# Attention layer: another order for the projections and the rotation of later heads, for the softmax's scaling and for the output projection

## The chip, the cores and the metric

The kernel runs on one NeuronCore of a Trainium2 chip. The metric is the device time of one execution in microseconds (us); of several runs the median is given. The engines are named PE (TensorE, matrix products, with its weight loads as PEld), DVE (VectorE), ACT (ScalarE), POOL (GpSimd) and SP (SyncE, which issues DMAs). L712 is line 712 of the kernel before.

## The reference

An encoder of two layers on a sequence of 512 tokens with 1024 features. Layer 0 mixes tokens by gated linear attention, layer 1 by grouped-query softmax attention; each is followed by a gated MLP with a width-3 convolution (2816 hidden features). The change lies in layer 1's attention alone:

```python
def attn_mixer(h, w_qkv, q_norm, k_norm, w_out, cos, sin):
    proj = h @ w_qkv                     # 8 query heads, 2 key heads, 2 value heads of 128
    q, k, v = split and reshape proj
    q = apply_rope(rmsnorm(q, q_norm), cos, sin)
    k = apply_rope(rmsnorm(k, k_norm), cos, sin)
    # per block of 128 queries and per head (4 query heads share one key head)
    s = einsum('bkgqd,bksd->bkgqs', q_blk, k) * scale
    p = softmax(s, axis=-1)
    o = einsum('bkgqs,bksd->bkgqd', p, v)
    return o @ w_out

def apply_rope(x, cos, sin):
    x1, x2 = x[..., :half], x[..., half:]
    return concatenate([x1 * cos - x2 * sin, x1 * sin + x2 * cos], axis=-1)
```

All in float32.

## The kernel before

Activations are held with features on the 128 partitions and the 512 tokens along the free axis, x as 8 such tiles. Every large product is made of three matmuls (`mm3`, L239 to L243): both factors are split into a rounded high part and the rest, and high x high, high x low and low x high are summed in PSUM.

**Weights.** `Weights` (L98 to L138) hands out halves of 128 x 1024 elements. A half needs its raw data from HBM (L113, an SP DMA of 1 MB for two halves, two buffers), then two casts on ACT (L118 for the high part, L119 for its negative) and an accumulating DMA issued by POOL (L120) that adds the raw data to the latter, which gives the low part. `half` also makes the next half of a fixed list ahead. There are three buffers for the high and three for the low parts.

**A pair of heads.** `roped` (L609 to L635) projects two heads at once into PSUM banks A and B, A holding the first halves of both heads, B the second: 2 x 8 steps of one `mm3`. Then the squares (L615, L616), their sum (L617), `scale_tok` (L594 to L607: a small matmul L598 into hs, on DVE L602, L181, a power on POOL L185, and L605 gives a scale per token and head), the four products with the norm's weight and cos or sin (L623), and per head a subtract on DVE (L630) and an add on POOL (L631), each on 64 partitions, into the rotated tile ry. `qpair` (L663) splits ry into high and low part (ACT L638, DVE L639). `kpair` (L648) does the same for the keys, with the scale multiplied in. `roped`, `kpair` and `qpair` are generators: each `yield` is a point at which the caller may go on with something else. For the keys and the query pair 0 these steps lie between each other and the value projection (L676 to L692).

**The blocks.** Query heads 0 to 7 times 4 blocks of 128 queries make 32 blocks t. In the loop at L754:

- `scores(t)`: 3 matmuls into one of two banks "s", row maximum (DVE L712), its negative scaled (L713), the exponential with its row sum (ACT L715), the reciprocal (L716) and the scaling of p by it (L717).
- a filler: 4 steps (`F_STEPS`) of the query pair that comes next, so pair 1 is prepared in blocks 0 to 7, pair 2 in 8 to 15, pair 3 in 16 to 23; what is left of a pair is done ahead of its first block (L757 to L759).
- `turn(t - 4)`: four PE transposes of p (L729) and the copy to high and low part (ACT L732, DVE L733).
- `mix(t - 6)` on every second block: p times v, 12 matmuls of 256 columns, into "po"; after a head's second, the head's output is split (oT, L638 and L639).

**The output projection** `out_steps` (L276 to L308) has a step of six matmuls (L292) per pair of output tiles and head. Of its first two groups the heads 0 to 5 come first (12 steps); the heads 6 and 7 follow, then groups 2 and 3. Before, these 12 steps are put into the loop from block 31 on, three in a block, the rest behind the loop.

The program's order is not the order on the engines: instructions are put in order per engine by a scheduler of the framework, with the program's order as the priority, and it may pull ready work ahead. Each engine then works through its list in that order and waits on semaphores.

PSUM has 8 banks: "acc" 3, "s" 2, "pt" 2, "po" 1. In SBUF "g" has 22 big buffers (128 x 1024), "t" 6 small ones (128 x 512; p and ry are there), "u" 4 (the four products of L623).

Of the kernel before, what the change touches and what calls it, by code (L numbers as in the profile page):

```python
# [1 line left out]

# [5 lines left out]
F32 = mybir.dt.float32  # L8
# [3 lines left out]
ALU = mybir.AluOpType  # L12

P = 128
S = 512
# [6 lines left out]
QH, HD = 8, 128  # L22
# [5 lines left out]

GATE_STEPS, GATE_LAG = (0, 2, 5, 7, 10, 12, 15, 17), 2

F_STEPS = 4
LAGS = (4, 6)


PC_NORM = 0
# [6 lines left out]
def hybrid_encoder_kernel(  # L42
# [21 lines left out]
    pe, act, dve, pool, sync = nc.tensor, nc.scalar, nc.vector, nc.gpsimd, nc.sync  # L64
# [8 lines left out]
    def nm(s):  # L73
        uid[0] += 1
        return f"{s}{uid[0]}"
# [9 lines left out]
    def big(dt, n):  # L85
        return pair("g", 22, dt, n)

    def tmp(tag, n, w=S):
        return sp.tile([P, w], F32, tag=tag, bufs={"u": 4, "t": 6, "sq": 3}[tag], name=nm(n))
# [63 lines left out]
    for c in range(KC):  # L153
        sync.dma_start(x[c], xT[c * P : (c + 1) * P, :])
        r = slice((c % 4) * S, (c % 4 + 1) * S)
# [120 lines left out]
    def out_steps(src, hl, nxt):  # L276


        pss, ws = {}, {}

        def part(ng, ks):
            if ng not in pss:
                pss[ng] = [bank("s" if ng % 2 else "acc", "op") for _ in range(2)]
            for k in ks:
                hf, kk = divmod(k, 4)
                if (ng, hf) not in ws:
                    ws[ng, hf] = W.half(src, ng * 2 + hf)
                wh, wl = ws[ng, hf]
                for i, (wt, mv) in enumerate(((wh, hl[k][0]), (wh, hl[k][1]), (wl, hl[k][0]))):
                    for n in range(2):  # L290
                        sl = slice((kk * 2 + n) * P, (kk * 2 + n + 1) * P)
                        mm(pss[ng][n], wt[:, sl], mv, start=k == 0 and i == 0, stop=k == KC - 1 and i == 2)  # L292
                yield

        def end(ng):
            for n in range(2):
                c = ng * 2 + n
                dve.tensor_tensor(x[c], x[c], pss[ng][n], ALU.add)
                nxt.chunk(c)

        yield from part(0, range(6))
        yield from part(1, range(6))
        for ng in range(2):
            yield from part(ng, (6, 7))
            end(ng)
        for ng in (2, 3):
            yield from part(ng, range(KC))
            end(ng)  # L308
# [278 lines left out]
    def attention(norm, nxt):  # L587
# [3 lines left out]
        cos, sin = cs[:, :S], cs[:, S:]  # L591
        r2 = cp.tile([P, NT], F32, name="r2")

        def scale_tok(sq, extra, keep):  # L594

            ps = bank("pt", "hs")
            for j in range(NT):
                mm(ps[:, 2 * j : 2 * j + 2], sq[:, j * P : (j + 1) * P], bd, start=True, stop=True)  # L598
            t = tiny(8, "hs", "tiny2")
            t3 = t.rearrange("p (j e) -> p j e", e=2)  # L600
            bc = lambda a: a.rearrange("p (j o) -> p j o", o=1).to_broadcast([P, NT, 2])
            dve.tensor_tensor(t3, ps[:, :8].rearrange("p (j e) -> p j e", e=2), bc(r2), ALU.mult)  # L602
            r = rsqrt_eps(t, 8, "hr", tag="tiny2")
            o = cp.tile([P, 8], F32, name=nm(keep))
            dve.scalar_tensor_tensor(o.rearrange("p (j e) -> p j e", e=2), r.rearrange("p (j e) -> p j e", e=2),  # L605
                                     extra, bc(norm.rtok), ALU.mult, ALU.mult)
            return o  # L607

        def roped(i, wcol, extra, keep, tag="acc"):  # L609

            pa, pb = bank(tag, "A"), bank(tag, "B")
            yield from feature_steps(*W.half(qk_order[i], 0), norm.hl, pa)
            yield from feature_steps(*W.half(qk_order[i], 1), norm.hl, pb)
            qa, qb = tmp("sq", "qa"), tmp("sq", "qb")
            act.activation(qa, pa, AF.Square)  # L615
            act.activation(qb, pb, AF.Square)  # L616
            dve.tensor_tensor(qa, qa, qb, ALU.add)  # L617
            yield
            sc = scale_tok(qa, extra, keep)
            wa, wb = prm[:, wcol : wcol + 1], prm[:, wcol + 1 : wcol + 2]  # L620
            t = [tmp("u", "rt") for _ in range(4)]
            for dst, src, w, tab in ((t[0], pa, wa, cos), (t[1], pb, wb, sin), (t[2], pa, wa, sin), (t[3], pb, wb, cos)):
                dve.scalar_tensor_tensor(dst, src, w, tab, ALU.mult, ALU.mult)  # L623
                if tag == "acc" and keep == "qsc":
                    yield
            res = []
            for e in range(2):
                r = slice(64 * e, 64 * e + 64)
                y = tmp("t", "ry")
                dve.tensor_tensor(y[0:64, :], t[0][r, :], t[1][r, :], ALU.subtract)  # L630
                pool.tensor_tensor(y[64:128, :], t[2][r, :], t[3][r, :], ALU.add)  # L631
                res.append(y)
                if tag == "acc" and keep == "qsc":
                    yield
            return res, sc  # L635

# [4 lines left out]
        def whole(gen):  # L641
            while True:
                try:
                    next(gen)
                except StopIteration as e:
                    return e.value

        def kpair():  # L648
            ky, ksc = yield from roped(0, PC_QK + 2, 1.0, "ksc")
            kk = []  # L650
            for e in range(2):
                if e == 0:
                    yield
                ps = bcast_rows([ksc[:, 2 * j + e : 2 * j + e + 1].to_broadcast([P, P]) for j in range(NT)])
                dve.tensor_tensor(ky[e], ky[e], ps, ALU.mult)
                t = big(F32R, "k")
                split(ky[e], t)
                kk.append(t)
            return kk
# [3 lines left out]
        def qpair(i, tag="acc"):  # L663
            ys, sc = yield from roped(1 + i, PC_QK, HD ** -0.5, "qsc", tag)
            for e in range(2):
                t = big(F32R, "q")
                split(ys[e], t)
                if tag == "acc" and e == 0:
                    yield
                heads[2 * i + e] = (t, sc, e)  # L670

        def run(gen, n):
            for _ in range(n):
                next(gen)

        kg, qg = kpair(), qpair(0, "s")  # L676
# [1 line left out]
        norm.tokens()  # L678
        dve.tensor_tensor(r2, norm.rtok, norm.rtok, ALU.mult)
        run(qg, 4)  # L680
        run(kg, 1)
        run(qg, 2)
        run(kg, 1)
        run(qg, 8)
        kk = whole(kg)
        run(qg, 2)

        ps = [bank("acc" if j < 2 else "pt", "av") for j in range(NT)]
        vg2 = token_steps(w_av, 0, norm.hl, ps, 2 * HD, 4)
        run(vg2, 4)  # L690
        whole(qg)
        whole(vg2)  # L692
        vh, vl = big(F32R, "vh"), big(F32R, "vl")
# [7 lines left out]
        probs, pts, pos = {}, {}, {}  # L701

        def scores(h, j):

            qt, sc, e = heads[h]
            kt = kk[h // 4]
            js = slice(j * P, (j + 1) * P)
            s = bank("s", "s")
            mm3(s, qt[:, js], qt[:, S + j * P : S + (j + 1) * P], kt[:, :S], kt[:, S:], True, True)
            scj = sc[:, 2 * j + e : 2 * j + e + 1]  # L710
            mx, nb, sm, rc = (tiny(1, n) for n in ("mx", "nb", "sm", "rc"))
            dve.reduce_max(mx, s, axis=mybir.AxisListType.X)  # L712
            dve.tensor_scalar(nb, mx, scj, -1.0, ALU.mult, ALU.mult)  # L713
            p = tmp("t", "p")
            act.activation(p, s, AF.Exp, scale=scj, bias=nb, accum_out=sm)  # L715
            dve.reciprocal(rc, sm)  # L716
            dve.tensor_scalar(p, p, rc, None, ALU.mult)  # L717
            probs[h, j] = p
# [28 lines left out]
                oh[h] = (t[:, :S], t[:, S:])  # L747

        LAG, LAG2 = LAGS
        early = 0  # L750
        blocks = [(h, j) for h in range(QH) for j in range(NT)]
        filler = qpair(1)
        osteps = out_steps(w_aout, oh, nxt)
        for t in range(len(blocks) + LAG2):  # L754
            if t < len(blocks):
                h, j = blocks[t]
                if j == 0 and h % 2 == 0 and h:  # L757
                    whole(filler)
                    filler = qpair(h // 2 + 1) if h < 6 else None  # L759
                scores(h, j)  # L760
                if filler is not None:
                    for _ in range(F_STEPS):
                        next(filler, None)
            if LAG <= t < len(blocks) + LAG:
                turn(*blocks[t - LAG])
            if t >= LAG2:
                h, j = blocks[t - LAG2]
                if j % 2 == 1:
                    mix(h, j // 2)
                    if h == 5 and j == 3:  # L770
                        early = 12
            if t >= len(blocks) - 1 and early:
                n = min(early, 3)
                run(osteps, n)
                early -= n
        run(osteps, early)
        whole(osteps)

    norms = [Norm(i) for i in range(4)]
# [85 lines left out]
```

## Time and profile before

| what | value |
|---|---|
| median of 3 runs (1144.7 to 1145.62) | 1145.59 us |
| the profiled execution | 1145.94 us |
| its span, first to last instruction | 1144.2 us |
| granted TensorE clock | 1.00 |
| attention layer in the trace | about 605 to 779 us |

The operations of the blocks and of the preparation, as the profile groups them:

| line, engine | what | count | mean us |
|---|---|---|---|
| L712 DVE | row maximum of s | 32 | 0.676 |
| L713 DVE | its negative, scaled | 32 | 0.207 |
| L715 ACT | exponential | 32 | 0.777 |
| L716 DVE | reciprocal | 32 | 0.159 |
| L717 DVE | scaling of p | 32 | 0.481 |
| L732 ACT, L733 DVE | transposed p, high and low part | 32, 32 | 0.595, 0.683 |
| L617 DVE | sum of squares | 5 | 0.685 |
| L623 DVE | product with weight and cos or sin | 20 | 0.744 |
| L630 DVE | subtract of the rotation | 10 | 1.319 |
| L631 POOL | add of the rotation | 10 | 1.514 |
| L185 POOL | power, 8 columns (hr) | 5 | 1.665 |
| L638 ACT, L639 DVE | split of a query head | 8, 8 | 0.632, 0.794 |
| L292 PE | output projection | 384 | 0.394 |

The profile's matmul durations overlap, since matmuls are pipelined; what one adds to the time is read from the start of one to the start of the next. Idle time in brackets behind a row of a timeline is that of the engine ahead of the row, with what ended it. In the chain of waits each step is followed back from the last instruction to what released it, or to the instruction before it on its engine.

### The profile page before, as it was taken

How to read it: one execution, taken by the hardware profiler on the slowest of the kernel's cores; microseconds unless marked ns; L12 is line 12 of the kernel's file. 1: busy time of each engine (PE TensorE's matmuls, PEld its weight loads, DVE VectorE, ACT ScalarE, POOL GpSimd, SP SyncE). 2: the span in 40 equal slices, each digit the busy share in tenths (PEclk: the TensorE clock that was granted, in tenths of full speed). 3: DMA queues.
4: the chain of work that ended last, by engine and by line, in shares of the span. 5: the costliest groups of instructions: out<-in, count | busy, mean ns of one | idle time of the engine just before them, and what ended most of it. 6: DMA issues, size and time to landing. Idle time of an engine off the chain costs nothing.

```text
span 1144.2 us, 13055 instructions
## 1 busy us (share of the span) xinstructions
PE 1131.9 (99%) x5280; PEld 942.3 (82%) x5280; DVE 688.3 (60%) x998; ACT 485.9 (42%) x695; POOL 80.6 (7%) x71
## 2 busy tenths in 40 slices
PE   9999999999999999999999999999999999999998
PEld 7888888888888888888888878888888888888887
DVE  5667653577777777633326688846777777762221
ACT  6465233444444444422244666654444444441210
POOL 0214110000000000000004322010000000000000
PEclk9999999999999999999999999999999999999999
DMA  6322211222322323323256633253322322323320
GB/s 228 135 86 74 78 70 38 74 104 81 111 82 103 111 74 111 110 74 111 97 148 161 148 74 74 56 112 111 111 101 83 111 83 101 111 76 126 129 92 19
DMA packets 20412, 113.76 MB, mean 99 GB/s; under 512 B 2432, under 2 KB 2816, under 8 KB 8832
## 3 DMA queue, kind: packets, MB, share of 16 engines
q1 hardware_dynamic: 17328, 102.42, 25.8%
q0 software_dynamic: 2880, 10.49, 4.8%
q8 instruction: 41, 0.67, 0.2%
q14 instruction: 19, 0.16, 0.0%
q10 hardware_dynamic: 144, 0.02, 0.0%
HBM read 100.34 MB, written 2.10 MB: 90 GB/s over the span
## 4 chain that ended last, share of the span: by engine, by line
PE 90%; issue 4%; DVE 3%; POOL 1%; DMA 1%; ACT 0%; SPq 0%; POOLq 0%; ACTq 0%
PE up L243 14%; PE up L242 14%; PE up L241 14%; PE dn L242 7%; PE dn L241 7%; PE dn L243 7%; PE op L292 5%; PE vg L267 2%; PE vg L269 2%; PE vg L268 2%; PE o L504 2%; PE kv L483 1%; PE B L241 1%; PE B L243 1%; PE B L242 1%
## 5 line engine op out<-in xcount | busy, mean ns | idle before, releaser
L129 ACT ACTIVATE wh<-raw 128x1024 fp32r<-128x1024 f32 x160 | 168.8, 1056 | 335.1 <-PE up L242 132.3
L130 DVE TENSOR_TENSOR wl<-raw,wh 128x1024 fp32r<-128x1024 f32 x160 | 199.0, 1244 | 149.8 <-ACT wh L129 149.4
L241 PE MATMUL up<-xhl,wh 128*128 128x512 f32 x704 | 274.3, 390 | 0.0
L243 PE MATMUL up<-xhl,wl 128*128 128x512 f32 x704 | 274.0, 389 | 0.0
L242 PE MATMUL up<-xhl,wh 128*128 128x512 f32 x704 | 273.9, 389 | 0.0
L242 PEld LDWEIGHTS up<-xhl,wh 128*128 128x128 f32 x704 | 132.2, 188 | 27.5
L241 PEld LDWEIGHTS up<-xhl,wh 128*128 128x128 f32 x704 | 132.1, 188 | 27.5
L243 PEld LDWEIGHTS up<-xhl,wl 128*128 128x128 f32 x704 | 132.1, 188 | 27.3
L243 PE MATMUL dn<-gu,wl 128*128 128x512 f32 x352 | 137.0, 389 | 0.0
L241 PE MATMUL dn<-gu,wh 128*128 128x512 f32 x352 | 137.0, 389 | 0.0
L242 PE MATMUL dn<-gu,wh 128*128 128x512 f32 x352 | 137.0, 389 | 0.0
L559 DVE TENSOR_TENSOR u<-up,R 128x512 f32<-128x512 f32 x88 | 60.3, 687 | 52.6 <-PE up L243 52.5
L561 ACT ACTIVATE y<-u,cw 128x512 f32<-128x512 f32 x88 | 71.1, 810 | 21.6 <-DVE u L559 21.6
L241 PEld LDWEIGHTS dn<-gu,wh 128*128 128x128 f32 x352 | 66.1, 188 | 13.8
L243 PEld LDWEIGHTS dn<-gu,wl 128*128 128x128 f32 x352 | 66.1, 188 | 13.8
L242 PEld LDWEIGHTS dn<-gu,wh 128*128 128x128 f32 x352 | 66.1, 188 | 13.5
L292 PE MATMUL op<-oT,wh 128*128 128x512 f32 x256 | 71.1, 394 | 0.0
L563 DVE SCALAR_TENSOR_TENSOR y<-u,cw,y 128x511 f32<-128x511 f32 x88 | 65.9, 751 | 2.9
L562 DVE SCALAR_TENSOR_TENSOR y<-u,cw,y 128x511 f32<-128x511 f32 x88 | 65.5, 746 | 0.6 <-ACT y L561 0.6
L565 ACT ACTIVATE y<-y 128x512 f32<-128x512 f32 x44 | 27.9, 634 | 87.8 <-DVE y L563 87.8
L292 PEld LDWEIGHTS op<-oT,wh 128*128 128x128 f32 x256 | 47.5, 188 | 9.7 <-ACT oT L519 0.3
L267 PE MATMUL vg<-wh,xhl 128*128 128x512 f32 x128 | 50.4, 399 | 0.1
(189 smaller groups left out, 1517.7 us busy)
## 6 DMA issues: line engine op xcount, KB each, us to landing
raw<-in_w_up_dram SPq DMA_DIRECT2D x44, 1024.0 KB, 4.7
raw<-in_w_down_dram SPq DMA_DIRECT2D x22, 1024.0 KB, 4.8
wl<-raw POOLq DMA_DIRECT2D x20, 512.0 KB, 4.7
raw<-in_w_vg_dram SPq DMA_DIRECT2D x6, 1024.0 KB, 4.8
raw<-in_w_akq_dram SPq DMA_DIRECT2D x5, 1024.0 KB, 5.1
raw<-in_w_kq_dram SPq DMA_DIRECT2D x4, 1024.0 KB, 4.7
raw<-in_w_gout_dram SPq DMA_DIRECT2D x4, 1024.0 KB, 4.7
raw<-in_w_aout_dram SPq DMA_DIRECT2D x4, 1024.0 KB, 4.9
```

Source lines behind the costliest of these rows:

```text
L129: act.activation(hi[:, sl], r[:, sl], AF.Copy)
L130: dve.tensor_tensor(lo[:, sl], r[:, sl], hi[:, sl].bitcast(F32), ALU.subtract)
L241: mm(ps, wh, mh, start=start, stop=False)
L242: mm(ps, wh, ml, start=False, stop=False)
L243: mm(ps, wl, mh, start=False, stop=stop)
L267: mm(ps[j][:, :width], xh, wh[:, sl], start=st, stop=False)
L292: mm(pss[ng][n], wt[:, sl], mv, start=k == 0 and i == 0, stop=k == KC - 1 and i == 2)
L559: dve.tensor_tensor(u, ps, norm.R, ALU.mult)
L561: act.activation(y, u, AF.Identity, scale=w(1), bias=w(3))
L562: dve.scalar_tensor_tensor(y[:, 1:], u[:, : S - 1], w(0), y[:, 1:], ALU.mult, ALU.add)
L563: dve.scalar_tensor_tensor(y[:, : S - 1], u[:, 1:], w(2), y[:, : S - 1], ALU.mult, ALU.add)
L565: act.activation(res[1], res[1], AF.Silu)
```

## The change

Six edits, all in `attention`:

1. The filler is replaced by a plan by block: the 16 projection steps of pair 1 lie in blocks 0 to 4, of pair 2 in 5 to 11, of pair 3 in 12 to 19 (`Q_STEPS`); the ten steps of preparation in blocks 5 to 8, 12 to 16 and 20 to 24 (`Q_READY`).
2. `roped` gives up control more often; the four products come ahead of `scale_tok`, the two from bank A first among them.
3. The rotation's subtract goes to POOL for the query pairs 1 to 3; for the keys and pair 0 it stays on DVE.
4. The rotated tile comes from the "g" buffers: one 128 x 1024 tile in place of two 128 x 512 tiles of "t".
5. Reciprocal and scaling of p become `shares(t)`, put behind `turn` in the same block.
6. The first 12 steps of the output projection are put into blocks 22 to 37 one at a time (`O_STEPS`).

With them the calls that weave the keys, pair 0 and the value projection are counted anew for the added yields.

```diff
-F_STEPS = 4
 LAGS = (4, 6)
+Q_STEPS = {1: (0, (4, 3, 3, 3, 3)), 2: (5, (3, 2, 2, 2, 2, 2, 3)), 3: (12, (2,) * 8)}
+Q_READY = {1: (5, (4, 3, 2, 1)), 2: (12, (3, 3, 2, 1, 1)), 3: (20, (3, 3, 2, 1, 1))}
+O_STEPS = (22, 24, 25, 27, 29, 31, 32, 33, 34, 35, 36, 37)
...
             dve.tensor_tensor(qa, qa, qb, ALU.add)
             yield
-            sc = scale_tok(qa, extra, keep)
             wa, wb = prm[:, wcol : wcol + 1], prm[:, wcol + 1 : wcol + 2]
             t = [tmp("u", "rt") for _ in range(4)]
-            for dst, src, w, tab in ((t[0], pa, wa, cos), (t[1], pb, wb, sin), (t[2], pa, wa, sin), (t[3], pb, wb, cos)):
+            for dst, src, w, tab in ((t[0], pa, wa, cos), (t[2], pa, wa, sin), (t[1], pb, wb, sin), (t[3], pb, wb, cos)):
                 dve.scalar_tensor_tensor(dst, src, w, tab, ALU.mult, ALU.mult)
-                if tag == "acc" and keep == "qsc":
-                    yield
-            res = []
+                yield
+            sc = scale_tok(qa, extra, keep)
+            yield
+            res = big(F32, "ry")
+            res = [res[:, :S], res[:, S:]]
+            sub = dve if tag == "s" or keep == "ksc" else pool
             for e in range(2):
                 r = slice(64 * e, 64 * e + 64)
-                y = tmp("t", "ry")
-                dve.tensor_tensor(y[0:64, :], t[0][r, :], t[1][r, :], ALU.subtract)
-                pool.tensor_tensor(y[64:128, :], t[2][r, :], t[3][r, :], ALU.add)
-                res.append(y)
-                if tag == "acc" and keep == "qsc":
+                sub.tensor_tensor(res[e][0:64, :], t[0][r, :], t[1][r, :], ALU.subtract)
+                pool.tensor_tensor(res[e][64:128, :], t[2][r, :], t[3][r, :], ALU.add)
+                if e == 0:
                     yield
...
-        run(kg, 1)
+        run(kg, 5)
         run(qg, 2)
-        run(kg, 1)
+        run(kg, 3)
         run(qg, 8)
         kk = whole(kg)
         run(qg, 2)
...
-        run(vg2, 4)
+        run(qg, 5)
+        run(vg2, 3)
         whole(qg)
         whole(vg2)
...
             act.activation(p, s, AF.Exp, scale=scj, bias=nb, accum_out=sm)
+            probs[h, j] = (p, sm, rc)
+
+        def shares(h, j):
+            p, sm, rc = probs[h, j]
             dve.reciprocal(rc, sm)
             dve.tensor_scalar(p, p, rc, None, ALU.mult)
             probs[h, j] = p
...
+        plan = collections.defaultdict(list)
+        for i in range(1, QH // 2):
+            g = qpair(i)
+            for first, counts in (Q_STEPS[i], Q_READY[i]):
+                for t, n in enumerate(counts):
+                    plan[first + t] += [g] * n
+        for t in O_STEPS:
+            plan[t].append(osteps)
         for t in range(len(blocks) + LAG2):
             if t < len(blocks):
-                h, j = blocks[t]
-                if j == 0 and h % 2 == 0 and h:
-                    whole(filler)
-                    filler = qpair(h // 2 + 1) if h < 6 else None
-                scores(h, j)
-                if filler is not None:
-                    for _ in range(F_STEPS):
-                        next(filler, None)
+                scores(*blocks[t])
+            for g in plan[t]:
+                next(g, None)
             if LAG <= t < len(blocks) + LAG:
                 turn(*blocks[t - LAG])
+            if t < len(blocks):
+                shares(*blocks[t])
             if t >= LAG2:
                 h, j = blocks[t - LAG2]
                 if j % 2 == 1:
                     mix(h, j // 2)
-                    if h == 5 and j == 3:
-                        early = 12
-            if t >= len(blocks) - 1 and early:
-                n = min(early, 3)
-                run(osteps, n)
-                early -= n
-        run(osteps, early)
         whole(osteps)
```

More of the change, by code (lines that the diff above doesn't have):

```diff
@@ L1 @@
+import collections
 from contextlib import ExitStack
@@ L651, in kpair @@
             for e in range(2):
-                if e == 0:
-                    yield
+                yield
                 ps = bcast_rows([ksc[:, 2 * j + e : 2 * j + e + 1].to_broadcast([P, P]) for j in range(NT)])
@@ L665, in qpair @@
             for e in range(2):
+                yield
                 t = big(F32R, "q")
                 split(ys[e], t)
-                if tag == "acc" and e == 0:
-                    yield
                 heads[2 * i + e] = (t, sc, e)
@@ L749, in attention @@
         LAG, LAG2 = LAGS
-        early = 0
         blocks = [(h, j) for h in range(QH) for j in range(NT)]
-        filler = qpair(1)
         osteps = out_steps(w_aout, oh, nxt)
+        plan = collections.defaultdict(list)
[6 more added lines that the diff above has]
+            plan[t].append(osteps)
         for t in range(len(blocks) + LAG2):
             if t < len(blocks):
-                h, j = blocks[t]
-                if j == 0 and h % 2 == 0 and h:
-                    whole(filler)
-                    filler = qpair(h // 2 + 1) if h < 6 else None
-                scores(h, j)
-                if filler is not None:
-                    for _ in range(F_STEPS):
-                        next(filler, None)
+                scores(*blocks[t])
+            for g in plan[t]:
+                next(g, None)
             if LAG <= t < len(blocks) + LAG:
                 turn(*blocks[t - LAG])
+            if t < len(blocks):
+                shares(*blocks[t])
             if t >= LAG2:
```

## The prediction

> **What bounds the kernel now.** First the page's busy times, then the busy times by 10 us windows of the attention layer, then the chain of waits, then the timelines of TensorE (PE), VectorE (DVE) and GpSimd (POOL) around the holes that the chain names.
>
> ```profile
> PE 1131.9 (99%) x5280; PEld 942.3 (82%) x5280; DVE 688.3 (60%) x998; ACT 485.9 (42%) x695; POOL 80.6 (7%) x71
> ```
>
> PE is never short of work for long, so only time in which PE starts no matmul can be won. The attention layer runs from 605 to 779 us. The window view (columns: window, its length, then busy us and count on PE, weight load, DVE, ACT, POOL; clock, DMA share, GB/s) shows where it is short:
>
> ```profile
> 640.00:650.00 10.00, 10.00 (x53) 8.24 (x52) 6.70 (x18) 7.18 (x12) 1.72 (x2) 1.00 0.62 149
> 650.00:660.00 10.00, 8.59 (x48) 6.63 (x45) 9.22 (x17) 4.39 (x9) 4.57 (x3) 1.00 0.37 86
> 680.00:690.00 10.00, 8.47 (x46) 6.59 (x45) 9.94 (x19) 4.46 (x9) 2.91 (x2) 1.00 0.00 0
> 700.00:710.00 10.00, 10.00 (x69) 8.95 (x68) 6.83 (x18) 5.80 (x10) 2.52 (x2) 1.00 0.59 159
> 710.00:720.00 10.00, 8.49 (x51) 6.79 (x50) 9.48 (x19) 5.21 (x11) 2.89 (x2) 1.00 0.00 0
> ```
>
> Three times DVE is nearly full (9.2 to 9.9 of 10) while PE drops to 8.5, and next to each lies a window in which DVE has 3 us free. That is unevenness, not a lack of DVE. The four PE pieces that end a hole (timeline of PE):
>
> ```profile
> 660.02 0.44 PE L729 MATMUL pt<-ident,p 128*128 128x128 f32 x2 [1.32 <-DVE ptl L733]
> 686.50 0.39 PE L241 MATMUL po<-pth,vh 128*128 128x256 f32 x1 [1.39 <-DVE oT L639]
> 715.79 0.39 PE L241 MATMUL po<-pth,vh 128*128 128x256 f32 x1 [1.36 <-DVE oT L639]
> 769.10 0.73 PE L292 MATMUL op<-oT,wl 128*128 128x512 f32 x2 [0.63 <-DMA wl<-raw]
> ```
>
> The brackets understate the loss, since ends of matmuls are modelled. From start to start, a 512-column matmul in a dense stretch takes 0.2275 us, a 256-column one 0.12, a transpose 0.11. The matmul before 660.02 started at 658.31, so 1.71 - 0.23 = 1.48 us is lost; in the same way 1.55 (684.72 to 686.50), 1.52 (714.04 to 715.79) and 0.79 (768.08 to 769.10). Shorter waits lose 0.26 at 653.51, 0.31 at 681.56 and 0.31 at 710.64. **Losses in all: 4.55 + 0.88 + 0.79 = 6.22 us.** Summed over every matmul from 640 to 780 the excess is 9.55; the other 3.3 lies in steps under 0.25 us between different kinds of matmul, whose number the change leaves alone.
>
> What DVE does before the first hole (timeline of DVE):
>
> ```profile
> 653.86 1.35 DVE L630 TENSOR_TENSOR ry<-rt,rt 64x512 f32<-64x512 f32 x1
> 655.14 0.15 DVE L716 RECIPROCAL rc<-sm 128x1 f32<-128x1 f32 x1
> 655.32 1.60 DVE L630 TENSOR_TENSOR ry<-rt,rt 64x512 f32<-64x512 f32 x1
> 656.96 0.48 DVE L717 TENSOR_SCALAR p<-p,rc 128x512 f32<-128x512 f32 x1
> 657.36 0.68 DVE L639 TENSOR_TENSOR q<-ry,q 128x512 fp32r<-128x512 f32 x1
> ```
>
> This is the rotation of a pair of heads: the two subtracts L630, then the splits L639, all in one lump, and the ptl (L733) for which PE waits at 660.02 stands behind them. The chain of waits runs from 647.98 to 660.02 through DVE and one GpSimd power, without PE.
>
> **The change, part by part.**
>
> *Projections spread (the plan by query block).* The same 48 matmuls a pair, 48 x 0.2275 = 10.9 us, the same weights. Cost nothing: PE is dense on either side. The loads, casts and accumulating DMAs move with the steps that ask for them: each half weight is an SP load (landing 5.1 us), two ACT casts (1.06 + 1.05) and a GpSimd issue (0.86, landing 4.7), 8 us once the load is there, and it can now queue behind up to four rotation operations on GpSimd (4 x 1.6 = 6.5). It is asked for eight steps ahead, some 3.5 blocks of about 3.4 us = 12 us, and three buffers let the casts run further ahead (the cast at 645.57 serves matmuls that start at 678.57), so I take nothing; without that cover 14.5 - 12 = 2.5 us a half.
>
> *Steps of the preparation.* The four scaled products (L623) come before the power chain and singly. The products are 4 x 0.74 = 3 us of DVE; the power chain (hs 0.99 on PE, 1.67 on GpSimd) starts up to that much later, but its result is wanted only by the head's first scores, two blocks (7 us) on. Nothing.
>
> *Subtract on GpSimd.* Six L630 leave DVE: 3 x (1.35 + 1.60) = 8.9 us, 2.95 of it ahead of each hole, which is more than the hole's 1.5. GpSimd gets two more operations a pair at 1.27 to 1.63 us (the adds, L631): four in a row, 5.1 to 6.5 us. Placed as before, with the last product done at 653.22, the first head's rotation would end after two of them, at 655.8 to 656.5; its split stood at 657.36. So the head is no later, and products done earlier by the plan make it earlier.
>
> *Shares later.* The reciprocal and the scaling of p come behind the transposed tile's ptl of the same block. DVE stood idle ahead of the reciprocal for 12.9 us in 15 places, waiting for the exponential; these now hold no ptl. No instruction is saved. Worth nothing by itself, it helps to empty the holes. What is late next is p, which its transposes want only four blocks later.
>
> *Rotated tile in the big pool.* By the program at most 18 of 22 big buffers are live in the block loop; two of six small buffers come free for p. Nothing, or a little of the 0.31 waits.
>
> *Output projection from block 22.* 12 steps of 6 matmuls, 16.4 us, the same work. The trace has output matmuls from 707.88 on already, though the program puts them into block 31: instructions are put on the engines in another order than the program's, ready work being pulled ahead. Nothing. The 0.79 at 769 stays: that half's buffer is freed only late, and 2.1 of casts + 0.9 + 7.9 of DMA stand against 48 x 0.2275 = 10.9 us of matmuls.
>
> **Sum.** The profiled execution took 1145.94 us (span 1144.2), 0.35 over the median of the runs. Removed: 4.55 + 0.88 = 5.43. What of a hole remains is not shown by any row: at best nothing, at worst all (1.5 a pair) or more (below). The nearest rows are the short waits at the same places, 0.26 to 0.31; I take a little more, 0.4 a pair, 1.2 in all. 1145.94 - 5.43 + 1.2 = 1141.7, or 1141.4 against the median: **1141.5 us**. All holes gone, the tail's and 0.5 of the small steps too, gives 1138.9.
>
> **Rivals.**
>
> *It does not do what it says: no change (1145.6).* Since ready work is pulled ahead anyway (the products of a pair at 640.59, long before their turn), a finer program order may give nearly the same engine orders, with holes at other places. For it: the output matmuls at 707.88. Against it: in none of the three places did that reordering save the lump, and the subtracts really leave DVE. Half the gain or less, 1143.3 to 1147.5.
>
> *Slower: GpSimd blocks DVE.* Place: each pair's run of rotation on GpSimd. While GpSimd adds, a DVE operation on SBUF data does not run (timelines of GpSimd and of DVE, at the keys' rotation):
>
> ```profile
> 610.15 3.28 POOL L631 TENSOR_TENSOR ry<-rt,rt 64x512 f32<-64x512 f32 x2 [1.68 <-DVE rt L623]
> ```
>
> ```profile
> 610.97 1.31 DVE L630 TENSOR_TENSOR ry<-rt,rt 64x512 f32<-64x512 f32 x1
> 612.30 1.16 DVE L181 TENSOR_SCALAR hr<-hs 128x8 f32<-128x8 f32 x1
> 626.81 2.40 DVE L639 TENSOR_TENSOR q<-ry,q 128x512 fp32r<-128x512 f32 x2
> ```
>
> L630 takes 0.67 undisturbed; the 8-element L181, 0.16 elsewhere, ends only when GpSimd does at 613.43; the two L639 take 2.40 where 2 x 0.69 is usual. In the changed kernel the scaling of p (L717, two of them in 6.5 us) and one split can be held, each for up to 1.6 us: 4.9 us a pair at most, 2.4 if each is held half. Against that DVE is rid of 2.95. It decides once more than 2.95 a pair is lost: at 4.9 the hole grows from 1.5 to 3.4, three times 1.9 more, 1145.6 + 5.8 = 1151.4; half of that, 1148.5, is typical. Against it: ptl and the maximum read PSUM and were not held (L733 at 653.26: 0.68), and DVE has 3 us free in the windows between.
>
> The Trainium skill says of this, in "GPSIMD Engine Reference", section "1. Specifications", that GpSimd's SBUF interfaces are shared with VectorE, with contention for DVE instructions in a two-port mode or with two SBUF inputs. By that rule the scaling of p would be held too if it runs in such a mode; the trace shows it only for L630, L639 and L181, and no L717 met a rotation here.
>
> **How the numbers follow.** A measurement of this kernel tells 0.2% (2.3 us) from no change. Forecast case (1139 to 1143.3): 0.62. No change (to 1147.5): 0.20. GpSimd blocks DVE: 0.18. Faster 0.62, same 0.20, slower 0.18. The range takes in both sides, 1139.0 to 1148.0; the forecast's own is 1139.0 to 1143.3.
>
> **What would show it.** Right: no PE gap of 1.3 us after DVE between 650 and 720, L630 four times rather than ten on DVE, DVE under 9 of 10 in every window of the blocks, the wait before 769 still there. Wrong: PE waiting for a pair's split or first score (GpSimd late), or L717 and L639 at over 1 us under L631 (blocked), or new waits for weights behind GpSimd's queue.

## The result, and the profile after

The changed kernel took 1147.11 us (median of 20 runs, 1146.11 to 1149.29), the kernel before beside it 1145.68 us (20 runs): **ratio 1.0015, 95% interval 1.0008 to 1.0022**, 1.4 us more, which lies inside the 0.2% that count as no change. The profiled execution took 1146.72 us, its span is 1145.0.

Line numbers in a run's rows are those of its own kernel: L725 below is L717 of the kernel before, L636 and L637 its L630 and L631, L190 its L185. The page's first line and four windows of the blocks (columns as before):

```profile
PE 1131.7 (99%) x5280; PEld 942.3 (82%) x5280; DVE 683.7 (60%) x992; ACT 485.0 (42%) x695; POOL 87.5 (8%) x77
```

```profile
640.00:650.00 10.00, 10.00 (x50) 8.25 (x49) 7.74 (x19) 7.54 (x13) 0.87 (x1) 1.00 0.55 106
650.00:660.00 10.00, 8.12 (x51) 6.79 (x49) 6.79 (x16) 4.35 (x9) 7.76 (x6) 1.00 0.48 140
...
680.00:690.00 10.00, 9.95 (x60) 8.43 (x59) 6.84 (x18) 6.32 (x14) 5.53 (x4) 1.00 0.03 5
...
710.00:720.00 10.00, 7.89 (x46) 6.14 (x45) 6.82 (x17) 4.39 (x10) 2.33 (x2) 1.00 0.00 0
```

DVE, over 9 of 10 busy in the last three before, now has over 3 us free in each of them. The hole of pair 2 (680 to 690) is gone, but PE lost more at pairs 1 and 3, beside a DVE that is partly idle. The PE pieces that end a hole (timeline of PE):

```profile
660.79 0.50 PE L248 MATMUL s<-k,q 128*128 128x512 f32 x1 [2.68 <-DVE q L644]
...
714.26 0.33 PE L737 MATMUL pt<-ident,p 128*128 128x128 f32 x1 [1.35 <-DVE ptl L741]
715.34 0.50 PE L246 MATMUL s<-k,q 128*128 128x512 f32 x1 [0.75 <-ACT p L719]
...
769.91 0.73 PE L297 MATMUL op<-oT,wl 128*128 128x512 f32 x2 [1.00 <-DMA wl<-raw]
```

From start to start this is 2.85 us lost at pair 1 (1.48 before), 1.52 + 0.97 at pair 3 (1.52), none at pair 2 (1.55). The tail's DMA wait grew from 0.79 to 1.16. Together 1.37 + 0.97 - 1.55 + 0.37 = 1.16 us more. Against it, the three short waits that the prediction listed, 0.88, shrank to a single one of 0.37 (at 703.92). That leaves 0.65, near the 0.8 by which the two profiled executions differ (1146.72 and 1145.94); the rest of the 1.4 between the medians is not in these two traces (see the clock, at the end). Why DVE was late at pair 1, on the timelines of DVE and of GpSimd (rows left out at "..."):

```profile
652.37 1.57 DVE L725 TENSOR_SCALAR p<-p,rc 128x512 f32<-128x512 f32 x1
653.85 0.20 DVE L717 TENSOR_SCALAR nb<-mx,qsc 128x1 f32<-128x1 f32 x1
653.98 0.15 DVE L607 TENSOR_TENSOR hs<-hs,r 128x8 f32<-128x8 f32 x1
654.16 0.95 DVE L186 TENSOR_SCALAR hr<-hs 128x8 f32<-128x8 f32 x1
...
658.20 0.17 DVE L610 SCALAR_TENSOR_TENSOR qsc<-hr,rtok 128x8 f32<-128x8 f32 x1 [3.08 <-POOL hr L190]
658.28 0.68 DVE L741 TENSOR_TENSOR ptl<-pt,pth 128x512 fp32r<-128x512 f32 x1
...
660.06 0.68 DVE L644 TENSOR_TENSOR q<-ry,q 128x512 fp32r<-128x512 f32 x1
```

```profile
650.69 1.61 POOL L636 TENSOR_TENSOR ry<-rt,rt 64x512 f32<-64x512 f32 x1
652.37 1.28 POOL L637 TENSOR_TENSOR ry<-rt,rt 64x512 f32<-64x512 f32 x1
653.72 1.36 POOL L636 TENSOR_TENSOR ry<-rt,rt 64x512 f32<-64x512 f32 x1
655.14 1.28 POOL L637 TENSOR_TENSOR ry<-rt,rt 64x512 f32<-64x512 f32 x1
656.50 1.66 POOL L190 TENSOR_TENSOR hr<-hr,halfneg 128x8 f32<-128x8 f32 x1
```

Two things stand there. **Holding:** DVE operations on SBUF data take 1.57 (p, else 0.48) and 0.95 (eight columns, else 0.16), ending within 0.3 us of the end of a GpSimd operation. **Queueing:** the power L190 needs hr, which DVE has ready by 655.1, but it is the fifth in GpSimd's list and starts at 656.50; DVE stands 3.08 us at qsc, which needs it. Behind qsc in its list stand a ptl and, as the sixth, the split q of the head's queries, for which PE waits at 660.79; the whole rotation had been done by 656.42. At pair 3 the power again follows all four rotations (idle 2.45); at pair 2 it follows one (1.17), nothing is held, and the hole is gone.

From 640 to 745 us I call "held" the time of DVE's SBUF operations above a length just over their undisturbed one (0.70 for a rotation, 0.71 for a split, 0.51 for p, 0.20 for qsc, 0.18 for hr). Before: 4.66 us held, all in L630, and 1.80 idle at qsc. After: 3.38 held and 6.70 idle. The six subtracts took 8.87 us off DVE; the kernel paid 3.38 + (6.70 - 1.80) = 8.28 for it.

### The profile page after: what moved, and what is told of

Its sections match the earlier page's. It is cut to its first block, busy times and chain, and to the rows that moved or that the text cites. A ratio compares the mean times of both kernels' runs of the same rounds, so it can differ in the third digit from the quotient of the medians.

```text
span 1145.0 us, 13049 instructions
## 1 busy us (share of the span) xinstructions
PE 1131.7 (99%) x5280; PEld 942.3 (82%) x5280; DVE 683.7 (60%) x992; ACT 485.0 (42%) x695; POOL 87.5 (8%) x77
## 5 line engine op out<-in xcount | busy, mean ns | idle before, releaser
L125 POOL DMA_DIRECT2D wl<-raw x20 | 17.8, 888 | 461.9 <-ACT wl L124 461.9
```

What stands on the lines that cost most here:

```text
L125: pool.dma_start(lo.bitcast(F32), r, accum_op=ALU.add)
```

## The experiments

Two theories. **B, holding:** GpSimd's rotation with two inputs holds DVE's SBUF operations; what matters is how much GpSimd work lies beside DVE. **Q, queueing:** the power behind the rotations makes DVE wait in order at qsc; the rest would do what was forecast. Each kernel was timed against the kernel before on the same chip. In the table's order from a_pow_first on, the medians of the kernel before were 1146.01 (first four), 1145.96 (next four), 1145.16 (two) and 1145.95 (two).

| kernel | us | ratio, 95% interval | held | idle at qsc |
|---|---|---|---|---|
| before | 1145.7 | | 4.66 | 1.80 |
| after | 1147.11 | 1.0015, 1.0008 to 1.0022 | 3.38 | 6.70 |
| a_pow_first | 1147.11 | 1.0008, 0.9999 to 1.0016 | 6.56 | 1.86 |
| a_sub_dve | 1144.41 | 0.9986, 0.9977 to 0.9995 | 1.87 | 5.59 |
| a_sub_dve_pow_first | 1142.62 | 0.9969, 0.9958 to 0.9981 | 2.37 | 1.87 |
| b_sub_pool | 1148.07 | 1.0017, 1.0008 to 1.0026 | 6.90 | 2.33 |
| c_dummy | 1144.70 | 0.9991, 0.9982 to 1.0000 | 5.00 | 1.87 |
| c_all_dve | 1141.98 | 0.9968, 0.9957 to 0.9980 | 0 | 1.88 |
| b_all_dve | 1141.92 | 0.9969, 0.9958 to 0.9981 | 0 | 2.95 |
| b_shares | 1144.53 | 0.9995, 0.9986 to 1.0003 | 4.06 | 2.66 |
| a_all_dve | 1142.84 | 0.9978, 0.9970 to 0.9987 | 0 | 3.86 |
| b_all_dve_shares | 1143.81 | 0.9990, 0.9981 to 0.9999 | 0 | 3.12 |
| d_all_dve_dummy2 | 1152.75 | 1.0052, 1.0038 to 1.0066 | 8.57 | 3.15 |
| d_all_dve_dummy1 | 1146.17 | 1.0000, 0.9991 to 1.0008 | 1.97 | 5.30 |

Names with a start from the changed kernel, with b from the one before, with c from a_sub_dve_pow_first, with d from b_all_dve. "held" and "idle at qsc" are those of one profiled execution each. Executions also differ in when the attention layer begins, so where two traces are compared below I use "the stretch": from the start of PE's 2801st matmul (at 619 to 621 us) to that of its 5201st, the same work in every kernel. It took 502.53 us before and 503.12 in the changed kernel.

### The power ahead of the products (a_pow_first)

```diff
             t = [tmp("u", "rt") for _ in range(4)]
+            late = tag == "s" or keep == "ksc"
+            if not late:
+                sc = scale_tok(qa, extra, keep)
+                yield
             for dst, src, w, tab in (...):
...
-            sc = scale_tok(qa, extra, keep)
-            yield
+            if late:
+                sc = scale_tok(qa, extra, keep)
+                yield
```

> The changed kernel, but for query pairs 1 to 3 the scale chain (small matmul, power on GpSimd) is put ahead of the four products again; subtracts stay on GpSimd. Theory Q (the power stands behind four rotation operations in GpSimd's in-order queue, and DVE, in order too, stands at the qsc that wants it): power ahead of the rotations, DVE's waits for the power (3.1 and 2.5 us in pairs 1 and 3 of the changed kernel) shrink to 0.6 each, PE's holes of 2.85 and 1.52 + 0.97 go; 1147.1 - 4.5 = 1142.6, at most 1144. Theory B (GpSimd blocks DVE's operations on SBUF while it rotates: L725 at 1.57 and 1.07, the 8-element add at 0.95 and 1.16): the rotations are as many, the holes stay within 1 us: 1146 to 1147.5.

The queueing went (idle 6.70 to 1.86), the gain did not come: 1147.11 us. The held time doubled. Timeline of DVE at pair 1:

```profile
652.52 1.26 DVE L610 SCALAR_TENSOR_TENSOR qsc<-hr,rtok 128x8 f32<-128x8 f32 x1
...
654.36 1.02 DVE L730 TENSOR_SCALAR p<-p,rc 128x512 f32<-128x512 f32 x1
...
657.11 1.05 DVE L730 TENSOR_SCALAR p<-p,rc 128x512 f32<-128x512 f32 x1
```

The eight-column qsc (0.17) now runs beside the rotations and takes 1.26. This profiled execution was the slowest of its 11 runs and has a stretch of half clock (at the end), but the three runs at a mean clock of 1.000 took 1146.18 to 1146.71 too, so the clock does not hide the gain. Q alone is not enough.

### The subtracts back on DVE (a_sub_dve), and both (a_sub_dve_pow_first)

```diff
-            sub = dve if tag == "s" or keep == "ksc" else pool
+            sub = dve
```

> The changed kernel with the subtracts of all pairs on DVE again; the power still comes after the products, behind two adds rather than four rotations. Theory Q: the power is 2.6 us earlier in each of pairs 1 and 3, so DVE's wait for it is about 0.5 to 1 us, but DVE has the two subtracts to do there (2.95 a pair): holes about half, 1144.5 to 1146. Theory B: half the GpSimd time, but DVE's subtracts now collide with the adds as before: as the kernel before, 1145.7, or worse.

> The changed kernel with the subtracts on DVE and the scale chain ahead of the products for pairs 1 to 3: what is left is the spreading, the later shares, the big buffer and the output steps. If spreading and later shares were worth what was forecast without GpSimd's help: 1142 to 1143.5, with DVE under 9 of 10 at the three places. If the lump of DVE work only moves, as a third theory has it (the order on the engines is nearly the same whatever the program's order): holes of about 1.5 us at three places again, 1145 to 1146.

1144.41 and 1142.62 us. Against the changed kernel's 1.0015, undoing the third edit brings 0.9986, the intervals apart: that edit costs some 3 us where the forecast had it as the source of the gain. With the subtracts on DVE the power's place is worth another 1.8 us by the medians (the two intervals overlap a little) and 1.1 by the stretch (500.84 and 499.73). The other edits are then worth 3.4 us against before.

### The subtracts on GpSimd alone (b_sub_pool)

```diff
-                dve.tensor_tensor(y[0:64, :], t[0][r, :], t[1][r, :], ALU.subtract)
+                sub = dve if tag == "s" or keep == "ksc" else pool
+                sub.tensor_tensor(y[0:64, :], t[0][r, :], t[1][r, :], ALU.subtract)
```

> The kernel before with the subtracts of pairs 1 to 3 on GpSimd and nothing else. The power comes ahead of the rotations in GpSimd's queue here. Theory Q: DVE is rid of 2.95 us a pair and waits for nothing new, the three holes of 1.5 us shrink by more than half: 1142 to 1143.5. Theory B: DVE loses to GpSimd's four operations what it wins, 1145 to 1148.

1148.07, 2.1 us slower, with next to no queueing (idle 2.33). Timeline of DVE:

```profile
651.97 1.25 DVE L605 SCALAR_TENSOR_TENSOR qsc<-hr,rtok 128x8 f32<-128x8 f32 x1 [0.60 <-POOL hr L185]
...
656.27 1.28 DVE L718 TENSOR_SCALAR p<-p,rc 128x512 f32<-128x512 f32 x1
...
657.47 1.78 DVE L640 TENSOR_TENSOR q<-ry,q 128x512 fp32r<-128x512 f32 x1
```

Not the subtract but qsc, p and the split are held: 6.90 in place of 4.66. The operation has left DVE, the holding has not.

### GpSimd work that nobody reads (c_dummy)

```diff
+            spare = None if late else big(F32, "spare")
...
                 pool.tensor_tensor(res[e][64:128, :], t[2][r, :], t[3][r, :], ALU.add)
+                if not late:
+                    pool.tensor_tensor(spare[0:64, e * S : (e + 1) * S], t[0][r, :], t[1][r, :], ALU.subtract)
```

> The kernel with spreading, later shares, subtracts on DVE and the power ahead of the products (1142.6 us when it ran), plus two more subtracts a pair on GpSimd into a spare buffer that nothing reads; the instruction orders of PE, DVE and ACT are the same one by one. Theory B (holding): the only effect is that DVE's operations on SBUF are held while GpSimd works, 0.4 to 1.2 us each, one or two more a pair: DVE's held time grows by 1 to 2 us a pair and the time to 1143.8 to 1146.5. Theory Q (queue and late results on GpSimd): nobody waits for the extra work, and an add is 1.3 us later in pair 2 alone: 1142.6 to 1143.1.

The orders on PE, DVE and ACT are those of a_sub_dve_pow_first, instruction by instruction; only GpSimd has more to do. By the medians, from two chips, c_dummy took 2.08 us more for 2.63 us more held; by the stretch 1.73 more (501.46 against 499.73). (Its profiled execution, 1146.55, was the slowest of 11, and it came to the stretch 2.2 us later than the other.) The same DVE rows, first of a_sub_dve_pow_first, then of c_dummy:

```profile
655.91 0.69 DVE L641 TENSOR_TENSOR ry<-rt,rt 64x512 f32<-64x512 f32 x1
...
657.30 0.48 DVE L730 TENSOR_SCALAR p<-p,rc 128x512 f32<-128x512 f32 x1
```

```profile
658.11 1.08 DVE L642 TENSOR_TENSOR ry<-rt,rt 64x512 f32<-64x512 f32 x1
...
659.90 0.73 DVE L733 TENSOR_SCALAR p<-p,rc 128x512 f32<-128x512 f32 x1
```

### All rotation on DVE (c_all_dve, b_all_dve, a_all_dve)

In all three the adds of pairs 1 to 3 go to DVE, and the subtracts are there too; b_all_dve is the kernel before with this edit and no other:

```diff
-                pool.tensor_tensor(y[64:128, :], t[2][r, :], t[3][r, :], ALU.add)
+                (dve if tag == "acc" and keep == "qsc" else pool).tensor_tensor(y[64:128, :], t[2][r, :], t[3][r, :], ALU.add)
```

> The same kernel (1142.6) with the adds of pairs 1 to 3 on DVE too, so that GpSimd does no rotation in the blocks but the power. Theory B: four rotations of 0.67 a pair, 2.7 us, undisturbed, in place of two at up to 1.66 and 1.05 plus held scalings of p (0.87); DVE is no fuller, the holes of 1.13 and 1.07 shrink: 1140.5 to 1142. If DVE's load alone decides (two more instructions a pair, 1.3 us): 1143.5 to 1146.

> The kernel before with the adds of pairs 1 to 3 on DVE, the opposite of the change's third edit, and nothing else. Theory B: four times 0.67 = 2.7 us a pair on DVE in place of 1.35 + 1.60 = 2.95, nothing held: the same or 1 us faster, 1144.5 to 1146. If DVE's count of instructions decides: 6 x 0.67 = 4 us more, 1147 to 1150.

> The changed kernel with its third edit turned round: subtracts and adds of pairs 1 to 3 on DVE, the power still behind the products. Theory B: nothing holds DVE, and the power has GpSimd's queue to itself, so its late place in the program costs nothing: as the kernel with the power first and all rotation on DVE, 1141 to 1142.8. Theory Q in a wider form (the late power makes DVE stand at qsc whatever GpSimd does): DVE's waits at qsc stay at 1.5 to 2.5 us and the time at 1143.5 to 1145.

**b_all_dve took 1141.92 us**, c_all_dve 1141.98: the opposite of the third edit, alone, gives what was forecast for the whole change. DVE has six operations more and none is held (timeline of DVE and windows of b_all_dve):

```profile
653.55 0.67 DVE L630 TENSOR_TENSOR ry<-rt,rt 64x512 f32<-64x512 f32 x1
654.33 0.69 DVE L631 TENSOR_TENSOR ry<-rt,rt 64x512 f32<-64x512 f32 x1
```

```profile
650.00:660.00 10.00, 9.87 (x53) 7.63 (x52) 9.28 (x19) 5.12 (x9) 1.46 (x1) 1.00 0.33 75
...
680.00:690.00 10.00, 9.91 (x61) 8.42 (x60) 9.91 (x21) 8.28 (x15) 0.92 (x1) 1.00 0.21 39
...
710.00:720.00 10.00, 9.20 (x61) 7.79 (x60) 9.15 (x22) 7.20 (x15) 0.00 (x0) 1.00 0.00 0
```

DVE is as busy as before (9.28, 9.91, 9.15 of 10), yet PE has 9.87, 9.91, 9.20 where it had 8.59, 8.47, 8.49. So a full DVE alone does not make the holes. On this base the spreading, the order of the steps and the later shares add nothing: c_all_dve, which has them, is level with b_all_dve. a_all_dve keeps the power behind the products (idle 3.86) and lies 0.1% above c_all_dve, with overlapping intervals: what queueing is worth with nothing held, at most.

### The later shares alone (b_shares, b_all_dve_shares)

```diff
             act.activation(p, s, AF.Exp, scale=scj, bias=nb, accum_out=sm)
+            probs[h, j] = (p, sm, rc)
+
+        def shares(h, j):
+            p, sm, rc = probs[h, j]
             dve.reciprocal(rc, sm)
...
                 turn(*blocks[t - LAG])
+            if t < len(blocks):
+                shares(*blocks[t])
```

> The kernel before with the reciprocal and the scaling of p behind the transposed tile's ptl, and nothing else. As predicted it is worth little by itself: 1145 to 1146.5. If it alone empties the holes (ptl no longer behind a wait for the exponential): 1142 to 1144.

> The kernel before with the adds of pairs 1 to 3 on DVE and the later shares; the two edits gave 1141.9 and 1144.5 each alone, against 1146.0. If they add, 1140.5; the later shares helped by 1 to 1.5 us mainly where DVE was held, so with nothing held they should be worth 0 to 0.7: 1141.2 to 1142.

Inconclusive on the kernel before (1144.53, the interval takes in 1); on b_all_dve they lose rather than gain (0.9990 against 0.9969, on two chips, the intervals just touching). The stretches, one execution each, point the same ways: 501.38 against 502.53, and 500.60 against 498.49. No gain of the shares by themselves is shown, and why they lose on b_all_dve stays open.

### The dose (d_all_dve_dummy2, d_all_dve_dummy1)

```diff
+            spare = big(F32, "spare") if tag == "acc" and keep == "qsc" else None
...
+                if spare is not None:
+                    pool.tensor_tensor(spare[0:64, e * S : (e + 1) * S], t[0][r, :], t[1][r, :], ALU.subtract)
+                    pool.tensor_tensor(spare[64:128, e * S : (e + 1) * S], t[2][r, :], t[3][r, :], ALU.add)
```

This gives two unread operations per head, four a pair. In dummy1 the two lines are `pool.tensor_scalar(..., t[0][r, :], 1.0, None, ALU.mult)` and the same of t[2]: one input each.

> The kernel before with its adds of pairs 1 to 3 on VectorE (that version took 1141.92 us, nothing of VectorE was held), and beside them four GpSimd operations a pair (two subtracts, two adds, 64x512, two inputs each) whose result nobody reads. The orders of TensorE, VectorE and ScalarE are identical, instruction by instruction, to the version without them. If holding alone brings the lost time back (theory B), VectorE's operations on SBUF data beside them are lengthened by some 4 to 9 us over the three pairs and the time rises by 0.8 of that or less, to 1144 to 1149 us. If VectorE's load and order matter and GpSimd's operations do not, it stays at 1141.5 to 1142.5 us.

> The same, but the four unread GpSimd operations a pair have one input each (a copy with a factor, 64x512). Orders again identical. If any GpSimd operation on SBUF data holds VectorE, the same lengthening per microsecond of GpSimd as with two inputs, 1143 to 1149 us by its length. If only two inputs hold it, VectorE's durations stay at 0.68, 0.48 and 0.17 and the time at 1141.5 to 1142.5 us.

With two inputs 1152.75 us, 10.8 over b_all_dve at the same orders, more than either theory's bound; with one input 1146.17, 4.25 over. What lies beside each other, GpSimd's row first, then DVE's, in dummy2 and then in dummy1:

```profile
653.65 2.97 POOL L635 TENSOR_TENSOR spare<-rt,rt 64x512 f32<-64x512 f32 x2 [0.17 <-DVE rt L623]
```

```profile
654.20 1.25 DVE L631 TENSOR_TENSOR ry<-rt,rt 64x512 f32<-64x512 f32 x1
...
655.56 1.60 DVE L632 TENSOR_TENSOR ry<-rt,rt 64x512 f32<-64x512 f32 x1
```

```profile
654.33 1.49 POOL L634 TENSOR_SCALAR spare<-rt 64x512 f32<-64x512 f32 x1
655.90 1.74 POOL L635 TENSOR_SCALAR spare<-rt 64x512 f32<-64x512 f32 x1
```

```profile
654.79 0.69 DVE L631 TENSOR_TENSOR ry<-rt,rt 64x512 f32<-64x512 f32 x1
...
655.59 0.69 DVE L632 TENSOR_TENSOR ry<-rt,rt 64x512 f32<-64x512 f32 x1
```

About the same GpSimd time beside DVE (17.6 and 19.1 us of unread work) holds it for 8.57 us with two inputs and 1.97 with one. In dummy1 the other half of the price is queueing: idle at qsc rose by 5.30 - 2.95 = 2.35, and 1.97 + 2.35 = 4.32 stands against the measured 4.25. (At pairs 2 and 3 of dummy1 one L631 each is held, to 0.98.) In dummy2, 8.57 held leaves 2.3 of the 10.8. The windows behind one of its longer holes show more:

```profile
690.00:691.00 1.00, 1.00 (x10) 1.00 (x9) 1.00 (x4) 1.00 (x3) 0.00 (x0) 0.86 0.00 0
691.00:692.00 1.00, 1.00 (x6) 1.00 (x5) 1.00 (x3) 1.00 (x2) 0.00 (x0) 0.50 0.00 0
692.00:693.00 1.00, 1.00 (x5) 0.70 (x5) 1.00 (x4) 0.56 (x2) 0.89 (x1) 0.50 0.00 0
693.00:694.00 1.00, 1.00 (x5) 0.82 (x4) 0.91 (x3) 0.38 (x1) 0.03 (x1) 0.50 0.56 106
694.00:695.00 1.00, 1.00 (x8) 0.91 (x7) 0.69 (x1) 0.62 (x2) 0.00 (x0) 0.94 1.12 213
```

The third number from the end is TensorE's granted clock. Behind a hole of 2.10 us and one of 2.54 it fell to half for some 3.4 us each, and 3.4 us at half speed is 1.7 lost. The profiled execution, the slowest of five (1153.22), took 11.6 more than that of b_all_dve (1141.59); less twice 1.7 that leaves 8.2, so here too, as in c_dummy, a microsecond held cost PE somewhat less than one. The one run of this kernel at a mean clock of 1.000 took 1149.93, 8.0 over b_all_dve, which agrees; the other four, at 0.997 to 0.999, took 1151.78 to 1153.22.

## Why the prediction was wrong, point by point

*The spreading, the big pool and the output projection costed at nothing; the wait at 769 stays.* No new wait for a weight showed in the blocks, and the tail's wait stayed (1.16). Right, but for 0.4 us.

*"Subtract on GpSimd: 2.95 of it ahead of each hole, which is more than the hole's 1.5."* **This is the step that failed.** DVE did lose 8.87 us of busy time, but 4.66 of that was not work: it was L630 held by GpSimd's add. The work that could be moved was 6 x 0.70 = 4.2. With a second operation per head on GpSimd, others were held in its stead (p, hr, qsc, the split). The prediction read the same rows (L630 at 1.35 and 1.60 against 0.67 undisturbed) only as a risk to other operations, not as what the hole was made of. b_all_dve shows the reverse: take the rotation off GpSimd and 4 us come.

*"Steps of the preparation: its result is wanted only by the head's first scores. Nothing."* Failed too. The result is wanted late, but its consumer qsc stands in DVE's list well before that, and whatever follows it there waits. So "the head is no later" failed with it: the first split of pair 1 stood at 657.36 before and came at 660.06, although the rotation was done sooner, and the pair's first score waited for it, which the prediction had named as a sign of being wrong. The prediction counted GpSimd's queue for the rotation and the DMA issues, not for the power behind the rotations. Together with the added holding it took back the rest: idle 4.90 more.

*"DVE nearly full while PE drops. That is unevenness, not a lack of DVE."* A lack it was not, but spreading was not the cure: with DVE just as full and nothing held, the three PE windows stand at 9.2 to 9.9. What fits is that the order leaves no room for an operation that takes twice its length; that the scheduler plans with undisturbed lengths is an inference from c_dummy and dummy2 (same orders, longer operations, holes). No run shows its plan.

*"Sum: 0.4 a pair remains."* 5.43 us were to go; 2.85, 2.49 and 0 remain in the three places. The holes of pairs 1 and 3 are larger than before, pair 2's gain pays most of it back.

*The rival "GpSimd blocks DVE"* named the mechanism and p as its victim. Its threshold was about right: per pair 2.95 plus 0.60 of idle, 3.55, stood there before; pair 1 paid 1.83 held + 3.08 idle = 4.91 and lost 1.4 more on PE, pair 3 paid 3.99 and lost 1.0 more, pair 2 paid 1.17 and won 1.55. Its time, 1148.5, was for all three pairs held alike. *The rival "It does not do what it says"* gives the measured size, but not for its reason: the lump did move, and cost as much elsewhere. That the result lies near no change is a balance of these costs, not a sign that nothing happened.

The Trainium skill's rule cited there ("GPSIMD Engine Reference", "1. Specifications": contention with DVE instructions in a two-port mode or with two SBUF inputs) agrees with these rows: the split and qsc have two SBUF inputs and are held (1.78 and 1.25 in b_sub_pool). p and the eight-column hr have one tensor input and are held too (1.57, 0.95); that they run in a two-port mode is what the rule would need, and no trace here shows the mode. By it the forecast should have priced the third edit; it stood beside a rival instead.

## What to carry to other kernels

An idle engine is not free if its work lengthens that of the busy one: before an operation is moved to GpSimd, see whether DVE's rows beside GpSimd's rows are longer than elsewhere, and subtract that excess from what the move frees. Then look for what the moved operations stand in front of in GpSimd's list, and which consumer of it stands early in DVE's. Here the fastest version, level with c_all_dve, took elementwise work off GpSimd by one line of the kernel before: 1141.92 us, ratio 0.9969 (0.9958 to 0.9981).

## What the runs showed of the hardware

**Which DVE operations are held.** Beside a GpSimd rotation, which has two inputs of 512 columns: two-input ones on SBUF (rotation, split, qsc: 0.17 became 1.26) and one-input ones of 8 and 512 columns (hr, p). Not held in the same places: the one-column nb (0.20 at 653.85 while GpSimd worked) and operations that read PSUM (hs 0.15 at 653.98, ptl 0.69 at 650.94). Nor does GpSimd's power hold p, though it has two inputs (of 8 columns, 1.66 us): p took 0.48 at 650.72 beside it, in the kernel before. The Trainium skill ("Advanced Engine Details and Errata", "VectorE Performance Modes") says that GpSimd's instructions and DVE's two-port modes block each other, which need source and target in SBUF; the rows of p, hr and ptl agree with that. That a GpSimd operation with one input holds DVE so much less (1.97 against 8.57) is shown by the two dose runs alone.

**Holes above some 2 us can halve the clock.** It followed holes of 2.10 and 2.54 us in dummy2 and one of 2.29 in a_pow_first (0.50 from 712 to 715), but not one of 2.01 in b_sub_pool, nor the 2.85 us hole in the profiled execution of the changed kernel, so length alone does not decide. The Trainium skill ("TensorE: Matmul & The Clock Gate", "Part 1: The HAM clock gate (the 'warmup' mystery)") describes half the clock after an idle window of about 3.4 us that runs freely; the 3.4 us at 0.50 agree, an idle time of a full window does not, since the holes were shorter. Among the changed kernel's 20 runs the time goes with the mean granted clock: two at 1.000 took 1146.41 in the median, seven at 0.999 took 1146.86, seven at 0.998 took 1147.18, three at 0.997 took 1148.07, one at 0.996 took 1149.29; the kernel before was at 1.000 in 63 of its 87 runs beside the experiments and at 0.999 in the rest. The two at 1.000 are 0.7 above the kernel before's 1145.68, which fits the 0.65 that the holes of the trace give. So about half of the 1.4 us is probably this clock, behind the larger hole; no trace was taken of the runs at a lower one.
